# The moving columns of the projections read alternately from two halves of the tokens, in a two-layer decoder trunk

## The chip, the cores and the metric

The kernel runs on one core of one Trainium2 chip. The metric is the device time of one execution in microseconds (us); several runs are given by their median. A profile is one execution recorded by the hardware profiler, with the engines TensorE (PE for its matmuls, PEld for its weight loads), VectorE (DVE), ScalarE (ACT), GpSimd (POOL) and SyncE (SP, which issues the DMAs).

## The reference

16 learned tokens are put ahead of 256 given ones, so that 272 tokens of width 2048 go through two layers. Layer 0 mixes tokens by RWKV-7, layer 1 by gated linear attention (GLA); each is followed by a squared-ReLU MLP with 8192 hidden units. All of it is float32.

```python
h = concatenate([meta, x])                              # 272 x 2048
h = h + rwkv7_time_mix(rms_norm(h))                     # r, k, v, output: 2048 x 2048 each, and low-rank gates
h = h + square(relu(rms_norm(h) @ w1_0)) @ w2_0         # 2048 x 8192, 8192 x 2048
h = h + gla_time_mix(rms_norm(h))                       # w_in 2048 x 6160, w_o 2048 x 2048
h = h + square(relu(rms_norm(h) @ w1_1)) @ w2_1
out = rms_norm(h)[16:]
```

## The kernel before

Activations lie transposed: 128 features on the partitions and the tokens along the free dimension. A projection multiplies weight tiles of 128 by 128 (the stationary operand) with an activation tile (the moving operand, one column for each token) and adds up over the tiles of the contraction in one PSUM bank.

**Two parts of each number.** To keep float32 accuracy with the fast matmul type (`fp32r`), each operand is split into a rounded part and its remainder. An activation tile `x` or `h` is `[128, 2, 272]`: index 0 the rounded part, index 1 the remainder. `wload` (L127 to L139) brings 128 by 1024 weights, eight tiles, by DMA into one of three `raw` buffers; ACT rounds them into one of two `hi` buffers (L137), and DVE writes the remainder into one of two `lo` buffers (L138). One such load is called a group here. It is issued with a high priority, so that it stands early in the queues of SP, ACT and DVE; what it waits for is that the matmuls of the group two before are done with the buffer.

**Two forms of a projection.** `mm3` (L141 to L145, called by `proj`) takes three matmuls for each weight tile: `hi` by the rounded columns, `hi` by the remainder, `lo` by the rounded columns, mostly with all 272 tokens, into one bank of which 272 columns are used. `projw` (L161 to L173) is for the 256 tokens that remain needed late in the kernel. It takes two matmuls: `hi` by rounded part and remainder together, 2 times 256 columns, which fills the bank (L171), and `lo` by the 256 rounded columns (L172) on top of the first half of the bank. The two halves of the bank are added afterwards: by `joined` (ACT copies one half to SBUF, L180; DVE adds the other, L181) or by `addto` (two DVE additions into the residual `hres`, L186). All these matmuls read and write their columns one after the other. Two banks, both called `pj`, take turns.

**Stages in order of time.** The opening computes the first half of r, with eight banks at once, in an order written by hand (L338 to L431, `manual_schedule`). While its first inputs arrive, some matmuls on a tile of ones, `ar`, run into a bank `pu` that nobody reads (L340, and L351 to L360). They use several patterns of 512 moving columns. In L352 to L358 the 512 columns are cut into two halves, and the matmul reads `blk` columns from the first half, `blk` from the second, and so on in turn, for `blk` of 1, 4 and 16, three matmuls each; L360 reads 512 neighbouring columns, from column 1 on, three times:

```python
            for blk in (1, 4, 16):
                x = w[:, :512].rearrange("p (a b c) -> p b a c", a=2, c=blk)
                o = idle.rearrange("p (b a c) -> p b a c", a=2, c=blk)
                ...
                for _ in range(3):
                    nc.tensor.matmul(o, w[:, :128], x, start=True, stop=True)
            for _ in range(3):
                nc.tensor.matmul(idle, w[:, :128], w[:, 1:513], start=True, stop=True)
```

Up to about 640 us follow the rest of RWKV: r, the low-rank gates (`proj32` in plain float32, L198), k with the building of the recurrence's operands, then v and the output projection. The last two are cut into steps, and a hand-written order on TensorE interleaves them with the recurrence (`R(n)` runs n steps). The MLP of layer 0 (to about 1,310 us) is `proj` throughout, with all 272 tokens. GLA (to about 1,820 us) uses both forms, and the MLP of layer 1 (`up` L239, `down` L254) uses `projw`.

Of the kernel before, what the change touches and what calls it, by code (L numbers as in the profile page):

```python
# [13 lines left out]
ALU = mybir.AluOpType  # L14
# [6 lines left out]
KT = D // P  # L21
NMETA = 16
SEQ = 256
T = NMETA + SEQ
# [10 lines left out]
HK = 256  # L35
# [19 lines left out]
class Kern:  # L55
# [71 lines left out]
    def wload(self, src, prio=2000):  # L127
# [11 lines left out]
        return hi, lo  # L139

    def mm3(self, out, hi, lo, ws, xh, xl, first, last):  # L141
        nc = self.nc
        nc.tensor.matmul(out, hi[:, ws], xh, start=first, stop=False)  # L143
        nc.tensor.matmul(out, hi[:, ws], xl, start=False, stop=False)  # L144
        nc.tensor.matmul(out, lo[:, ws], xh, start=False, stop=last)  # L145

    def proj(self, srcs, x, n, off=0, bank=None):
        ps = bank() if bank else self.pj()
        nk = 8 * len(srcs)
        for i, s in enumerate(srcs):  # L150
            hi, lo = self.wload(s)
            for j in range(8):
                kt = 8 * i + j
                xt = x[kt]
                self.mm3(ps[:, :n], hi, lo, slice(j * P, (j + 1) * P), xt[:, 0, off : off + n],
                         xt[:, 1, off : off + n], kt == 0, kt == nk - 1)
        return ps[:, :n]

    def projw(self, srcs, x, off=0):  # L161
        nc = self.nc
        ps = self.pj()
        wide = ps.rearrange("p (a t) -> p a t", a=2)
        nk = 8 * len(srcs)
        for i, s in enumerate(srcs):
            hi, lo = self.wload(s)
            for j in range(8):
                kt = 8 * i + j
                ws = slice(j * P, (j + 1) * P)  # L170
                nc.tensor.matmul(wide, hi[:, ws], x[kt][:, :, off : off + SEQ], start=kt == 0, stop=False)  # L171
                nc.tensor.matmul(ps[:, :SEQ], lo[:, ws], x[kt][:, 0, off : off + SEQ], start=False, stop=kt == nk - 1)  # L172
        return ps[:, :SEQ], ps[:, SEQ:]  # L173


    def joined(self, pool, halves):
        nc = self.nc
        a, b = halves
        c = self.t(pool, [P, SEQ], "cj", 2)
        nc.scalar.copy(c, b)  # L180
        nc.vector.tensor_tensor(out=c, in0=a, in1=c, op=ALU.add)  # L181
        return c

    def addto(self, h, halves):
        for a in halves:
            self.nc.vector.tensor_tensor(out=h, in0=a, in1=h, op=ALU.add)  # L186
# [45 lines left out]
    def mlp(self, layer, x, rstd, hres, off, done):  # L232
        nc, tc, ap = self.nc, self.tc, self.ap
        n = T - off
        w1, w2 = ap[f"mlp_w1_{layer}"], ap[f"mlp_w2_{layer}"]
        with ExitStack() as es:
            hp = es.enter_context(tc.tile_pool(name=f"hid{layer}", bufs=1, side="right", reuse_waits="tile"))

            def up(b):  # L239
                hid = []  # L240
                for f in range(KT):
                    src = [w1[b * KT + f, i] for i in range(2)]
                    ps = self.joined(hp, self.projw(src, x)) if n == SEQ else self.proj(src, x, n)
                    z = self.t(hp, [P, T], "z", 2)[:, :n]
                    nc.vector.scalar_tensor_tensor(out=z, in0=ps, scalar=0.0, in1=rstd, op0=ALU.max, op1=ALU.mult)
# [24 lines left out]
    def rwkv(self, done):  # L270
        nc, tc, ap = self.nc, self.tc, self.ap
        tt = lambda o, a, b, op=ALU.mult: nc.vector.tensor_tensor(out=o, in0=a, in1=b, op=op)  # L272
        hres = self.hres
# [64 lines left out]
        with tc.manual_schedule(engines={ENG.PE, ENG.DVE, ENG.Activation}):  # L338
# [12 lines left out]
            w = warm.bitcast(F32R)  # L351
            for blk in (1, 4, 16):  # L352
                x = w[:, :512].rearrange("p (a b c) -> p b a c", a=2, c=blk)
                o = idle.rearrange("p (b a c) -> p b a c", a=2, c=blk)
                if blk == 1:
                    x, o = x[:, :, :, 0], o[:, :, :, 0]
                for _ in range(3):
                    nc.tensor.matmul(o, w[:, :128], x, start=True, stop=True)  # L358
            for _ in range(3):
                nc.tensor.matmul(idle, w[:, :128], w[:, 1:513], start=True, stop=True)  # L360
            om0 = self.one_minus(ep, "mix0")
# [34 lines left out]
            for kt in range(KT):  # L396
# [20 lines left out]
                for p in parts:  # L417
                    nc.scalar.copy(hi[:, p], raw[:, p])
                    if kt in (0, KT - 1):
                        low(w, p)  # L420
                xh, xl = xr[kt][:, 0], xr[kt][:, 1]
                for f in range(4):
                    nc.tensor.matmul(pss[f], hi[:, cols(f)], xh, start=kt == 0, stop=False)
                for f in range(4):
                    nc.tensor.matmul(pss[f], hi[:, cols(f)], xl, start=False, stop=False)
                    nc.tensor.matmul(pss[f], lo[:, cols(f)], xh, start=False, stop=kt == KT - 1)
                if kt in (0, KT - 1):
# [6 lines left out]
        for f in range(NR):  # L434
            nc.scalar.copy(rr[f], pss[f])
        xw = mix32(1, ep)
        xa = mix32(4, ep)
        tc.keep_in_program_order(nc.scalar.preload_act_table_set("sigmoid_and_others"))
        for f in (NR, NR + 1):
            nc.scalar.copy(rr[f], self.proj(pair(wr, f), xr, T))  # L440
        tw = self.t(e2, [P, T], "tw")
# [18 lines left out]
        for f in range(NR + 2, KT):  # L460
            nc.scalar.copy(rr[f], self.proj(pair(wr, f), xr, T))
# [81 lines left out]
        for f in range(KT):  # L543
# [7 lines left out]
            nc.scalar.activation(iW, ca[:, 0], AF.Exp, scale=DECAY)  # L551
            nc.scalar.mul(kk, ps, self.vec("k_k", f))
            nc.scalar.activation(sq, kk, AF.Square)
# [4 lines left out]
            nc.scalar.activation(sq, sq, AF.Exp, scale=-0.5)  # L558
            tt(kn, ps, kn)
            nc.vector.scalar_tensor_tensor(out=kk, in0=sq, scalar=1e12, in1=kk, op0=ALU.min, op1=ALU.mult)  # L560
# [228 lines left out]
        def v_proj(f):  # L789
            ps = self.pj()[:, :T]  # L790
            yield from units(xv, 2, ps)
            nc.scalar.copy(hres[:, f], ps)
            tt(rr[f], rr[f], hres[:, f])
            yield

        def outA(f):
            ps = self.pj()[:, :T]
            nc.sync.dma_start(loc[f], ap["hT"][:, f])
            yield from units(yo, 1, ps)
            tt(loc[f], ps, loc[f], ALU.add)  # L800
            yield


        def outQ(s, fp):
            hi, lo = weights.pop(0)
            pss = [self.pj()[:, :T] for _ in range(2)]
            for i in range(2):
# [3 lines left out]
                for j in range(4):  # L811
# [4 lines left out]
                    if j < 3:  # L816
                        yield
                tt(hres[:, f] if s == 3 else loc[f], pss[i], loc[f], ALU.add)
                if s == 3:
# [141 lines left out]
    def gla(self, x, rstd, hres, done):  # L961
# [16 lines left out]
        zf = self.t(gp, [P, T], "mn", 2)  # L978
        tt(zf, self.proj(pair(48), x, T), rstd)
        za = self.t(gp, [P, T], "za", 1, F32R)  # L980
# [6 lines left out]
        for hd in range(GH):  # L987
            Q = self.t(gp, [P, 2, 7 * C], "Q", 2)
            KX = self.t(gp, [P, 2, 160 + 6 * C], "KX", 1)
            for dt in range(2):  # L990
# [24 lines left out]
                qf = self.t(gp, [P, SEQ], "qf", 2)  # L1015
                nc.vector.scalar_tensor_tensor(out=qf, in0=pq, scalar=HK ** -0.5, in1=rs, op0=ALU.mult, op1=ALU.mult)
                tt(q[:, : 3 * C], qf[:, : 3 * C], eb[:, c0:c3])
# [7 lines left out]
                ks = self.t(gp, [P, T], "ks", 2)  # L1025
                tt(ks, pk, rstd)
                kx = KX[:, dt]
# [14 lines left out]
            for v in range(4):  # L1042
                pv = self.proj(pair(16 + 4 * hd + v), x, T)
                vs = self.t(gp, [P, T], "vs", 2)
                tt(vs, pv, rstd)
                pt = self.ptr()
# [8 lines left out]
            def cols(x, i, n=1):  # L1055
                return x[:, i * C : (i + n) * C]
# [32 lines left out]
            for v in range(4):  # L1089
                j = 4 * hd + v  # L1090
                pg = self.joined(gp, self.projw(pair(32 + j), x, NMETA))
                gt = self.t(gp, [P, SEQ], "gt", 2)
                tt(gt, pg, rs)
                sg = self.t(gp, [P, SEQ], "sg", 2)
# [155 lines left out]
```

## Time and profile before

| | |
|---|---|
| median of 3 runs | 2545.72 us (2544.17 to 2549.93) |
| profiled execution | 2546.85 us, of which the span from first to last instruction is 2545.1 us |
| mean granted TensorE clock | 0.997 of full speed |
| busy, share of the span | matmuls 99%, weight loads 92%, DVE 65%, ACT 49%, POOL 0% |
| DMA | 455 MB, mean 179 GB/s |

Matmuls are pipelined: a row's duration (289 ns for 272 columns) is that of one instruction from end to end, while the next starts much sooner. The pace of TensorE is read from the distance of two starts, or from a stretch of time divided by the number of matmuls in it. In the rows of the view by windows, each engine's busy time is followed by its count of instructions; the last three figures are the granted clock, the share of DMA time and GB/s.

### The profile page before, as it was taken

The numbers are of one execution on the slowest core, as the hardware profiler recorded it, in microseconds if no ns is written. First come the engines' busy times: TensorE is split into PE (matmuls) and PEld (weight loads), VectorE is DVE, ScalarE is ACT, GpSimd is POOL, SyncE is SP. The second block draws the span as 40 slices with busy tenths as digits, with TensorE's granted clock in tenths as the row PEclk, the third lists the DMA queues.
The fourth block names the chain that finished last, engine by engine and source line by source line (L and its number), as shares of the span: only waits on it lengthen the run. The fifth ranks groups of instructions, "written<-read, shape, count | busy, mean of one in ns | idle before, by whom it ended". The sixth has DMA issues, their size and how long they took to land. (4 is left out here: it accounts for less than half of the span.)

```text
span 2545.1 us, 47169 instructions
## 1 busy us (share of the span) xinstructions
PE 2511.8 (99%) x19262; PEld 2337.6 (92%) x19262; DVE 1643.9 (65%) x2748; ACT 1243.6 (49%) x1951; POOL 6.7 (0%) x20
## 2 busy tenths in 40 slices
PE   9999999999999999999999999999999999999998
PEld 8889998899999999999999999998888888888887
DVE  8777986748555455455456688777666656656665
ACT  6366544555444344344344455545555435445344
POOL 0000000000000000000000000000000000000000
PEclk9999999999999999999999999999999999999999
DMA  6578854434555555555555554445555555555554
GB/s 208 167 233 277 264 153 141 129 103 155 175 177 175 175 177 179 174 175 177 178 175 181 166 169 155 157 149 182 184 189 190 187 187 190 189 186 188 191 188 160
DMA packets 160729, 455.29 MB, mean 179 GB/s; under 512 B 34112, under 2 KB 50624, under 8 KB 160512
## 3 DMA queue, kind: packets, MB, share of 16 engines
q1 hardware_dynamic: 160512, 452.27, 54.9%
q8 instruction: 151, 2.47, 0.4%
q14 instruction: 66, 0.54, 0.1%
HBM read 433.86 MB, written 18.35 MB: 178 GB/s over the span
## 5 line engine op out<-in xcount | busy, mean ns | idle before, releaser
L137 ACT CAST hi<-raw 128x1024 fp32r<-128x1024 f32 (+1 forms) x818 | 796.8, 981 | 1080.6 <-PE pj L144 589.8
L138 DVE TENSOR_TENSOR lo<-raw,hi 128x1024 fp32r<-128x1024 f32 (+1 forms) x818 | 926.7, 1140 | 583.5 <-ACT hi L137 574.7
L143 PE MATMUL pj<-x,hi 128*128 128x272 f32 x2240 | 660.4, 295 | 2.6 <-DVE hres L272 2.5
L145 PE MATMUL pj<-x,lo 128*128 128x272 f32 x2240 | 648.4, 289 | 1.0 <-DVE lo L138 0.9
L144 PE MATMUL pj<-x,hi 128*128 128x272 f32 x2240 | 646.7, 289 | 0.0
L171 PE MATMUL pj<-x,hi 128*128 128x512 f32 x1664 | 585.5, 395 | 2.2 <-DVE cj L181 1.5
L172 PE MATMUL pj<-x,lo 128*128 128x256 f32 x1664 | 468.3, 282 | 1.3 <-DVE lo L138 1.3
L143 PEld LDWEIGHTS pj<-x,hi 128*128 128x128 f32 x2240 | 422.5, 189 | 10.8 <-issue 4.4
L144 PEld LDWEIGHTS pj<-x,hi 128*128 128x128 f32 x2240 | 424.9, 190 | 3.2 <-issue 1.4
L145 PEld LDWEIGHTS pj<-x,lo 128*128 128x128 f32 x2240 | 421.9, 188 | 2.8 <-DVE lo L138 2.1
L171 PEld LDWEIGHTS pj<-x,hi 128*128 128x128 f32 x1664 | 312.5, 188 | 75.6 <-issue 2.1
L171 PE MATMUL pj<-h,hi 128*128 128x512 f32 x1008 | 352.9, 394 | 0.0
L172 PEld LDWEIGHTS pj<-x,lo 128*128 128x128 f32 x1664 | 313.4, 188 | 2.2 <-DVE lo L138 1.9
L143 PE MATMUL pj<-h,hi 128*128 128x272 f32 (+1 forms) x1040 | 299.2, 288 | 0.0
L145 PE MATMUL pj<-h,lo 128*128 128x272 f32 (+1 forms) x1040 | 298.4, 287 | 0.0
L144 PE MATMUL pj<-h,hi 128*128 128x272 f32 (+1 forms) x1040 | 298.1, 287 | 0.0
L172 PE MATMUL pj<-h,lo 128*128 128x256 f32 x1008 | 284.0, 282 | 0.0
L171 PEld LDWEIGHTS pj<-h,hi 128*128 128x128 f32 x1008 | 189.4, 188 | 43.4
L144 PEld LDWEIGHTS pj<-h,hi 128*128 128x128 f32 x1040 | 196.7, 189 | 0.0
L143 PEld LDWEIGHTS pj<-h,hi 128*128 128x128 f32 x1040 | 195.7, 188 | 0.0
L145 PEld LDWEIGHTS pj<-h,lo 128*128 128x128 f32 x1040 | 195.2, 188 | 0.0
L172 PEld LDWEIGHTS pj<-h,lo 128*128 128x128 f32 x1008 | 190.5, 189 | 0.0
(270 smaller groups left out, 2113.7 us busy)
## 6 DMA issues: line engine op xcount, KB each, us to landing
raw<-mlp_w_d SPq DMA_DIRECT2D x512, 512.0 KB, 3.4
raw<-gla_in_d SPq DMA_DIRECT2D x98, 512.0 KB, 3.3
raw<-w_rkv_d SPq DMA_DIRECT2D x80, 512.0 KB, 4.0
raw<-gla_o_d SPq DMA_DIRECT2D x32, 512.0 KB, 3.4
raw<-rw_oQ_d SPq DMA_DIRECT2D x24, 512.0 KB, 3.3
raw<-w_r_d SPq DMA_DIRECT2D x16, 512.0 KB, 3.4
ard<-ar SPq DMA_DIRECT2D x16, 288.0 KB, 3.7
bkd<-bk SPq DMA_DIRECT2D x16, 288.0 KB, 3.8
```

Source lines behind the costliest of these rows:

```text
L137: nc.scalar.copy(hi[:, h], raw[:, h])
L138: nc.vector.tensor_tensor(out=lo[:, h], in0=raw[:, h], in1=hi[:, h].bitcast(F32), op=ALU.subtract)
L143: nc.tensor.matmul(out, hi[:, ws], xh, start=first, stop=False)
L144: nc.tensor.matmul(out, hi[:, ws], xl, start=False, stop=False)
L145: nc.tensor.matmul(out, lo[:, ws], xh, start=False, stop=last)
L171: nc.tensor.matmul(wide, hi[:, ws], x[kt][:, :, off : off + SEQ], start=kt == 0, stop=False)
L172: nc.tensor.matmul(ps[:, :SEQ], lo[:, ws], x[kt][:, 0, off : off + SEQ], start=False, stop=kt == nk - 1)
```

## The change

Every projection in `fp32r` reads its moving columns woven: token 0, token n/2, token 1, token n/2 + 1 and so on, where n is 272 or 256. The distance of the two places is 136 or 128 elements (in the idle matmuls of L358 with `blk` of 1 it is 256). The results are written one after the other as they come, so that the tokens stand woven in the PSUM bank: those of the first half at the even columns, those of the second at the odd ones. Whoever reads the bank, on DVE or ACT, takes every second column, first the even and then the odd ones, and writes the tokens to SBUF in their usual order. No instruction is added or removed outside the idle matmuls, whose twelve patterns are replaced by twelve others. The instructions stand in the same order as before on all engines and queues.

```diff
+    def weave(x):
+        return x.rearrange("p (a t) -> p t a", a=2)
+    def pairs(x):
+        return x.rearrange("p (t a) -> p t a", a=2)
+    def back(x):
+        return x.rearrange("p (t a) -> p a t", a=2)
+    def two(x):
+        return x.rearrange("p (a t) -> p a t", a=2)
 
     def mm3(self, out, hi, lo, ws, xh, xl, first, last):
+        out, xh, xl = self.pairs(out), self.weave(xh), self.weave(xl)
         nc.tensor.matmul(out, hi[:, ws], xh, start=first, stop=False)
 ...
     def proj(self, srcs, x, n, off=0, bank=None):
-        return ps[:, :n]
+        return self.back(ps[:, :n])
 ...
     def projw(self, srcs, x, off=0):
-        wide = ps.rearrange("p (a t) -> p a t", a=2)
+        wide, one = ps.rearrange("p (s t a) -> p s t a", s=2, a=2), self.pairs(ps[:, :SEQ])
 ...
-                nc.tensor.matmul(wide, hi[:, ws], x[kt][:, :, off : off + SEQ], start=kt == 0, stop=False)
-                nc.tensor.matmul(ps[:, :SEQ], lo[:, ws], x[kt][:, 0, off : off + SEQ], start=False, stop=kt == nk - 1)
-        return ps[:, :SEQ], ps[:, SEQ:]
+                xt = x[kt][:, :, off : off + SEQ].rearrange("p s (a t) -> p s t a", a=2)
+                nc.tensor.matmul(wide, hi[:, ws], xt, start=kt == 0, stop=False)
+                nc.tensor.matmul(one, lo[:, ws], xt[:, 0], start=False, stop=kt == nk - 1)
+        return self.back(ps[:, :SEQ]), self.back(ps[:, SEQ:])
 
     def joined(self, pool, halves):
-        nc.scalar.copy(c, b)
-        nc.vector.tensor_tensor(out=c, in0=a, in1=c, op=ALU.add)
-        return c
+        c2 = self.two(c)
+        nc.scalar.copy(c2, b)
+        nc.vector.tensor_tensor(out=c2, in0=a, in1=c2, op=ALU.add)
+        return c2
 
     def addto(self, h, halves):
+        h = self.two(h)
         for a in halves:
             self.nc.vector.tensor_tensor(out=h, in0=a, in1=h, op=ALU.add)
 ...
-            for blk in (1, 4, 16):
-                x = w[:, :512].rearrange("p (a b c) -> p b a c", a=2, c=blk)
 ...
+            for x in (v.rearrange("p (a t) -> p t a", a=4), v.rearrange("p (a t c) -> p t a c", a=2, c=2),
+                      v.rearrange("p (b a t) -> p b t a", a=2, t=16), v.rearrange("p (t a) -> p a t", a=2)):
 ...
+                outs = [self.pairs(x) for x in pss[:4]]
+                xh, xl = self.weave(xh), self.weave(xl)
                 for f in range(4):
-                    nc.tensor.matmul(pss[f], hi[:, cols(f)], xh, start=kt == 0, stop=False)
+                    nc.tensor.matmul(outs[f], hi[:, cols(f)], xh, start=kt == 0, stop=False)
 ...
         for f in range(NR):
-            nc.scalar.copy(rr[f], pss[f])
+            nc.scalar.copy(self.two(rr[f]), self.back(pss[f]))
 ...
-                tt(vs, pv, rstd)
+                tt(self.two(vs), pv, self.two(rstd))
```

The other places where a result is taken out of PSUM (r, k, v, the output projection, the MLP's `z`, GLA's q, k, v and gate) change as the last two do.

More of the change, by code (lines that the diff above doesn't have):

```diff
@@ L139, in wload @@
         return hi, lo
+    @staticmethod
+    def weave(x):
+        return x.rearrange("p (a t) -> p t a", a=2)
+    @staticmethod
+    def pairs(x):
+        return x.rearrange("p (t a) -> p t a", a=2)
+    @staticmethod
+    def back(x):
+        return x.rearrange("p (t a) -> p a t", a=2)
+    @staticmethod
+    def two(x):
+        return x.rearrange("p (a t) -> p a t", a=2)
     def mm3(self, out, hi, lo, ws, xh, xl, first, last):
         nc = self.nc
+        out, xh, xl = self.pairs(out), self.weave(xh), self.weave(xl)
         nc.tensor.matmul(out, hi[:, ws], xh, start=first, stop=False)
@@ L244, in up @@
                     z = self.t(hp, [P, T], "z", 2)[:, :n]
-                    nc.vector.scalar_tensor_tensor(out=z, in0=ps, scalar=0.0, in1=rstd, op0=ALU.max, op1=ALU.mult)
+                    nc.vector.scalar_tensor_tensor(out=self.two(z), in0=ps, scalar=0.0, in1=self.two(rstd), op0=ALU.max,
+                                                   op1=ALU.mult)
                     s = self.t(hp, [P, T], "s", 2)[:, :n]
@@ L351, in rwkv @@
             w = warm.bitcast(F32R)
-            for blk in (1, 4, 16):
-                x = w[:, :512].rearrange("p (a b c) -> p b a c", a=2, c=blk)
-                o = idle.rearrange("p (b a c) -> p b a c", a=2, c=blk)
-                if blk == 1:
-                    x, o = x[:, :, :, 0], o[:, :, :, 0]
+            v = w[:, :512]
+            for x in (v.rearrange("p (a t) -> p t a", a=4), v.rearrange("p (a t c) -> p t a c", a=2, c=2),
+                      v.rearrange("p (b a t) -> p b t a", a=2, t=16), v.rearrange("p (t a) -> p a t", a=2)):
+                o = idle.rearrange("p (t a) -> p t a", a=x.shape[2]) if len(x.shape) == 3 else idle.rearrange(
+                    "p (t a c) -> p t a c", a=x.shape[2], c=x.shape[3])
                 for _ in range(3):
                     nc.tensor.matmul(o, w[:, :128], x, start=True, stop=True)
-            for _ in range(3):
-                nc.tensor.matmul(idle, w[:, :128], w[:, 1:513], start=True, stop=True)
             om0 = self.one_minus(ep, "mix0")
@@ L421, in rwkv @@
                 xh, xl = xr[kt][:, 0], xr[kt][:, 1]
+                outs = [self.pairs(x) for x in pss[:4]]
+                xh, xl = self.weave(xh), self.weave(xl)
                 for f in range(4):
-                    nc.tensor.matmul(pss[f], hi[:, cols(f)], xh, start=kt == 0, stop=False)
+                    nc.tensor.matmul(outs[f], hi[:, cols(f)], xh, start=kt == 0, stop=False)
                 for f in range(4):
-                    nc.tensor.matmul(pss[f], hi[:, cols(f)], xl, start=False, stop=False)
-                    nc.tensor.matmul(pss[f], lo[:, cols(f)], xh, start=False, stop=kt == KT - 1)
+                    nc.tensor.matmul(outs[f], hi[:, cols(f)], xl, start=False, stop=False)
+                    nc.tensor.matmul(outs[f], lo[:, cols(f)], xh, start=False, stop=kt == KT - 1)
                 if kt in (0, KT - 1):
@@ L439, in rwkv @@
         for f in (NR, NR + 1):
-            nc.scalar.copy(rr[f], self.proj(pair(wr, f), xr, T))
+            nc.scalar.copy(self.two(rr[f]), self.proj(pair(wr, f), xr, T))
         tw = self.t(e2, [P, T], "tw")
@@ L460, in rwkv @@
         for f in range(NR + 2, KT):
-            nc.scalar.copy(rr[f], self.proj(pair(wr, f), xr, T))
+            nc.scalar.copy(self.two(rr[f]), self.proj(pair(wr, f), xr, T))
             if f == NR + 2:
@@ L551, in rwkv @@
             nc.scalar.activation(iW, ca[:, 0], AF.Exp, scale=DECAY)
-            nc.scalar.mul(kk, ps, self.vec("k_k", f))
+            nc.scalar.mul(self.two(kk), ps, self.vec("k_k", f))
             nc.scalar.activation(sq, kk, AF.Square)
@@ L558, in rwkv @@
             nc.scalar.activation(sq, sq, AF.Exp, scale=-0.5)
-            tt(kn, ps, kn)
+            tt(self.two(kn), ps, self.two(kn))
             nc.vector.scalar_tensor_tensor(out=kk, in0=sq, scalar=1e12, in1=kk, op0=ALU.min, op1=ALU.mult)
@@ L791, in v_proj @@
             yield from units(xv, 2, ps)
-            nc.scalar.copy(hres[:, f], ps)
+            nc.scalar.copy(self.two(hres[:, f]), self.back(ps))
             tt(rr[f], rr[f], hres[:, f])
@@ L799, in outA @@
             yield from units(yo, 1, ps)
-            tt(loc[f], ps, loc[f], ALU.add)
+            tt(self.two(loc[f]), self.back(ps), self.two(loc[f]), ALU.add)
             yield
@@ L817, in outQ @@
                         yield
-                tt(hres[:, f] if s == 3 else loc[f], pss[i], loc[f], ALU.add)
+                tt(self.two(hres[:, f] if s == 3 else loc[f]), self.back(pss[i]), self.two(loc[f]), ALU.add)
                 if s == 3:
@@ L978, in gla @@
         zf = self.t(gp, [P, T], "mn", 2)
-        tt(zf, self.proj(pair(48), x, T), rstd)
+        tt(self.two(zf), self.proj(pair(48), x, T), self.two(rstd))
         za = self.t(gp, [P, T], "za", 1, F32R)
@@ L1015, in gla @@
                 qf = self.t(gp, [P, SEQ], "qf", 2)
-                nc.vector.scalar_tensor_tensor(out=qf, in0=pq, scalar=HK ** -0.5, in1=rs, op0=ALU.mult, op1=ALU.mult)
+                nc.vector.scalar_tensor_tensor(out=self.two(qf), in0=pq, scalar=HK ** -0.5, in1=self.two(rs), op0=ALU.mult,
+                                               op1=ALU.mult)
                 tt(q[:, : 3 * C], qf[:, : 3 * C], eb[:, c0:c3])
@@ L1025, in gla @@
                 ks = self.t(gp, [P, T], "ks", 2)
-                tt(ks, pk, rstd)
+                tt(self.two(ks), pk, self.two(rstd))
                 kx = KX[:, dt]
@@ L1092, in gla @@
                 gt = self.t(gp, [P, SEQ], "gt", 2)
-                tt(gt, pg, rs)
+                tt(self.two(gt), pg, self.two(rs))
                 sg = self.t(gp, [P, SEQ], "sg", 2)
```

## Prediction

> **What bounds the kernel now.** I read the page's busy times, the chain that ended last, the costliest groups, then single stages.
>
> ```profile
> PE 2511.8 (99%) x19262; PEld 2337.6 (92%) x19262; DVE 1643.9 (65%) x2748; ACT 1243.6 (49%) x1951; POOL 6.7 (0%) x20
> PEclk9999999999999999999999999999999999999999
> PE 32%; DVE 1%; ACT 0%; issue 0%; DVEq 0%
> PE pj L171 21%; PE pj L172 11%; DVE fin L1158 0%; DVE lo L138 0%; DVE sg L1097 0%; PE pj L144 0%; PE pj L145 0%; PE pj L143 0%; DVE gt L963 0%; DVE x L963 0%; PE pm L1153 0%; PE pry L1087 0%; PE pm L228 0%; DVE hres L1158 0%; DVEq L1245 0%
> L143 PE MATMUL pj<-x,hi 128*128 128x272 f32 x2240 | 660.4, 295 | 2.6 <-DVE hres L272 2.5
> L145 PE MATMUL pj<-x,lo 128*128 128x272 f32 x2240 | 648.4, 289 | 1.0 <-DVE lo L138 0.9
> L171 PE MATMUL pj<-x,hi 128*128 128x512 f32 x1664 | 585.5, 395 | 2.2 <-DVE cj L181 1.5
> L172 PE MATMUL pj<-x,lo 128*128 128x256 f32 x1664 | 468.3, 282 | 1.3 <-DVE lo L138 1.3
> L171 PE MATMUL pj<-h,hi 128*128 128x512 f32 x1008 | 352.9, 394 | 0.0
> ```
>
> TensorE is the bound: matmuls fill 99% of the span, the chain (followed back only as far as 32% of the span) consists of the two projection lines, and ahead of the projections it idles 0 to 2.6 us in all. The clock is full, so there is nothing to win there. What remains is the pace of a matmul.
>
> ```profile
> core 0: us, PE busy (x) PEld busy (x) DVE busy (x) ACT busy (x) POOL busy (x), PEclk, DMA share, GB/s
> 700.00:900.00 200.00, 200.00 (x1604) 200.00 (x1603) 104.01 (x122) 85.90 (x109) 0.00 (x0) 1.00 0.54 176
> 1900.00:2100.00 200.00, 200.00 (x1145) 174.67 (x1144) 122.25 (x163) 94.64 (x131) 0.00 (x0) 1.00 0.58 187
> ```
>
> From 700 to 900 us, in the MLP of layer 0, all matmuls have 272 columns: 200 us / 1604 = 124.7 ns each, 0.458 ns a column. From 1900 to 2100 us (MLP of layer 1) wide and narrow ones alternate: 2 x 200 / 1145 = 349.3 ns a pair of 512 and 256 columns, 0.455 ns a column.
>
> The trace holds a faster pace. The idle matmuls of the opening stream 512 columns each in four patterns; the rows give the start of one of each pattern.
>
> ```profile
> 11.88 0.59 PE L358 MATMUL pu<-ar 128*128 128x512 f32 x2
> 12.32 0.66 PE L358 MATMUL pu<-ar 128*128 128x512 f32 x2
> 13.07 0.64 PE L358 MATMUL pu<-ar 128*128 128x512 f32 x2
> 13.79 0.62 PE L360 MATMUL pu<-ar 128*128 128x512 f32 x2
> 14.02 0.63 PE L360 MATMUL pu<-ar 128*128 128x512 f32 x2
> ```
>
> At 11.88 starts the second of the three with `blk` of 1, at 12.32 the first with 4, at 13.07 the first with 16, at 13.79 and 14.02 two with neighbouring columns. So two woven matmuls took 0.44 us, 0.22 each (0.43 ns a column; the rounding of two starts leaves 0.215 to 0.225); three with runs of 4 took 0.75, 0.25 each; three with runs of 16 took 0.72, 0.24 each; one of neighbouring columns took 0.23. The pattern that the change gives to all projections is the fastest of the four.
>
> **The change part by part.** *272 columns.* The first two rows below count the L143 matmuls from 63 us on, 927 + 2436 = 3363; each belongs to an `mm3`, so there are 10,089 matmuls, and the opening's 16 weight tiles by 8 features by 3 add 384: 10,473.
>
> ```profile
> 63.00:640.00 577.00, 282.72 (x927) 175.28 (x926) 0.99 0.58 180
> 640.00:2545.00 1905.00, 701.09 (x2436) 458.09 (x2435) 1.00 0.54 178
> 120.00:640.00 520.00, 263.86 (x863) 163.34 (x863) 0.99 0.59 182
> 0.00:2545.00 2545.00, 938.16 (x2672) 501.87 (x2672) 1.00 0.55 179
> ```
>
> Scaled from 512 columns at 0.215 to 0.22 us, 272 would take 114 to 117 ns. A fixed part in each matmul would push this up and the weight load, one with every matmul, may set a floor. How short a load can get shows in the present narrow matmul:
>
> ```profile
> 2006.37 0.19 PEld L171 LDWEIGHTS pj<-h,hi 128*128 128x128 f32 x1
> 2006.49 0.19 PEld L172 LDWEIGHTS pj<-h,lo 128*128 128x128 f32 x1
> 2006.48 0.39 PE L171 MATMUL pj<-h,hi 128*128 128x512 f32 x1
> ```
>
> The load for the wide matmul starts at 2006.37 and that matmul starts 0.11 us later, so a load needs 0.12 at most. Bounds are 114 and 120 ns; I take 116, near the scaled value, since the columns are what sets today's pace. That is 8.7 ns by 10,473 = 91 us.
>
> *Pairs of 512 and 256.* The last row above counts 2672. The wide one goes to 216 ns. The narrow one scales to 108 to 110, and the load bounds it by 120; today it takes what 349.3 leaves beside some 231, about 118. I take 110. A pair then takes 326 ns, 23.3 less, by 2672 = 62 us. Together 153 us, if TensorE stays the bound everywhere.
>
> *RWKV, 120 to 640 us.* Of the 10,473, 3 x 863 = 2,589 lie here, worth 22.5 us. Here others are near their limits:
>
> ```profile
> 220.00:240.00 20.00, 19.96 (x154) 18.97 (x154) 13.63 (x32) 12.39 (x22) 0.00 (x0) 1.00 0.92 308
> 300.00:320.00 20.00, 20.00 (x173) 19.46 (x173) 19.45 (x45) 7.06 (x15) 0.00 (x0) 1.00 0.93 294
> 320.00:480.00 160.00, 152.94 (x2244) 138.16 (x2244) 113.72 (x282) 78.49 (x162) 3.33 (x6) 0.98 0.52 148
> ```
>
> At 300 us DVE is busy 19.45 of 20 us, at 220 us the DMA engines 92%, and from 320 us on the projections fill the waits of the recurrence, which shorter matmuls fill less well. Between all and nothing I take half: 11 us are lost.
>
> *Reading PSUM with a step of two.* No row shows this. It may cost nothing, even gain a little; as the other end I let every element count twice, by the DVE row with 512 elements from PSUM against the one with 256.
>
> ```profile
> L186 DVE TENSOR_TENSOR hres<-pj,hres 128x256 f32<-128x256 f32 x159 | 67.5, 425 | 52.5 <-PE pj L172 46.7 <-PE pj L145 3.2
> L272 DVE TENSOR_TENSOR S<-pu,WC 128x512 f32<-128x512 f32 x8 | 5.5, 684 | 4.2 <-PE pu L722 4.2
> 2006.57 1.05 ACT L137 CAST hi<-raw 128x1024 fp32r<-128x1024 f32 x1 [1.75 <-PE pj L171]
> 2006.68 0.89 DVE L186 TENSOR_TENSOR hres<-pj,hres 128x256 f32<-128x256 f32 x2 [0.61 <-PE pj L172]
> 2007.65 1.23 DVE L138 TENSOR_TENSOR lo<-raw,hi 128x1024 fp32r<-128x1024 f32 x1
> 2009.28 0.39 PE L171 MATMUL pj<-h,hi 128*128 128x512 f32 x1
> DVE hres L186 <- PE pj L172: 46.7, 79, 0.7
> ```
>
> That is 684 - 425 = 259 ns for each read. Most of it is covered: a bank is next written one projection (over 5 us) later, and DVE is idle 39% of the stage. The tight place is `down` with `projw`. There the two `addto` reads end at 2007.57, and `lo`, queued behind them, starts at 2007.65 when `hi` is ready; it ends at 2008.88 for a group that starts at 2009.28, a reserve of 0.40 us. The faster group takes 8 x 23.3 = 0.19 us of it, leaving 0.21, so at the present cost of a read nothing waits. With the doubled cost `lo` is late by 2 x 0.26 - 0.08 = 0.44: TensorE waits 0.23 us, 79 times (the last row), 18 us. I take 4 us, nearer to nothing, since the DVE fetches one element at a time as it is (259 ns for 256 elements). The Trainium skill warns here (Vector Engine (DVE) Microarchitecture Reference, section 5.2, Measured stream behaviour on trn2): a stream keeps its full pace in runs of at least two neighbouring words, and costs about 1.7 to 2.5 ns a column where each element hops, against 1.05. That was measured in SBUF; no run here shows it for PSUM. By it, as an estimate, a read would cost some 0.18 to 0.37 us more and the sum would lose 8 to 40 us here instead of 4.
>
> ACT's reads (L180, the r and v copies) have their cover in ACT's 51% idle time. The faster groups ask for 7% more weights a second, 187 to some 200 GB/s in the MLP, below the 308 at 220 us. The new idle matmuls run before the first inputs are ready and cost nothing.
>
> Sum: 2546.85 - 153 + 11 + 4 = 2409 us for the profiled execution; the median of the runs is 1.1 us below it, so **2408 us**.
>
> **The rivals.** *The weave does not hold at the new distance.* In the idle matmuls the two places lie 256 elements apart, here 136 or 128, and the tile there is small and always the same. If changing place costs here what it cost with runs of 4, a column takes 0.25 / 512 = 0.488 ns: 272 columns take 133 ns (8 more, 10,473 times: 84 us), a pair 375 (26 more, 2672 times: 68 us), and the kernel takes about 2700 us. The switch lies at 124.7 ns for 272 columns. Against it speaks that hopping after every column was the cheapest of the hopping patterns. The Trainium skill takes this side (Advanced Engine Details and Errata, Memory Cachelines): SBUF lines have 16 bytes, and a stream that goes to another line with each access pays a penalty. The trace does not agree, with 0.22 us woven against 0.23 of neighbours. 0.11.
>
> *The weight load is the floor.* With 120 ns for every load, 272 columns gain 4.7 ns (49 us) and a pair 349.3 - 216 - 120 = 13 (35 us): 84 less 15 is 69, or 2477 us. With a floor of 118 it would be 70 + 41 - 15 = 96, or 2450. For it: loads are busy 200 of 200 us in the MLP. Against it: that counts durations of 188 ns that overlap. 0.12.
>
> *The step-of-two reads are slow.* At the doubled cost 18 us instead of 4, and some 8 more in RWKV, where DVE is full (k and v, 32 reads by 0.26): about 2430 us. 0.2.
>
> *No change in pace:* the weave reads as neighbours do, 2545 us. 0.03.
>
> **How the numbers follow.** The forecast has 0.54; it and the slow reads, both faster, span from 2380 (all of the 153 us and a few more where a narrow matmul reaches 108) to some 2435. I carry the upper end to 2455 to take in the milder floor. What is left out: the weave failing, no change, and the harder floor, under 2 in 10. A difference of 0.2%, 5 us, is about what a measurement of this kernel can tell from none: its runs lie within 0.23%. Faster 0.86, same 0.03, slower 0.11.
>
> **What would show it.** In the MLP of layer 0 some 1,720 matmuls in 200 us instead of 1604, and in that of layer 1 some 1,227 instead of 1145. The `addto` row should stay near 425 ns; 684 would be the slow read, and PE would then show idle time ahead of L172 put down to `lo`. Fewer than 1604 matmuls in the first stretch would prove the forecast wrong by its main term; 1604 to 1660 would point to the load.

## The result, and the profile after

The changed kernel takes 2420.34 us (median of 4 runs, 2418.27 to 2422.38) against 2547.82 us of the kernel before beside it: a ratio of 0.949 with a 95% interval of 0.946 to 0.953, 5.1% faster. The forecast was 2408 us, in a range of 2380 to 2455.

First the page of the changed kernel: span, busy times, and the costliest matmul groups. Line numbers have moved: `mm3` is L160 to L162 now, `projw` L189 and L190, `addto` L206.

```profile
span 2419.9 us, 47169 instructions
PE 2371.1 (98%) x19262; PEld 2235.7 (92%) x19262; DVE 1640.0 (68%) x2748; ACT 1242.5 (51%) x1951; POOL 6.6 (0%) x20
PEclk9999999999999999999999999999999999999999
PE pj L189 21%; PE pj L190 10%; DVE fin L1180 0%; DVE lo L138 0%; DVE sg L1119 0%; PE pj L161 0%; PE pj L160 0%; PE pj L162 0%; DVE gt L984 0%; DVE x L984 0%; PE pm L1175 0%; PE pm L248 0%; PE pry L1109 0%; DVE hres L1180 0%; DVEq L1267 0%
L162 PE MATMUL pj<-x,lo 128*128 128x272 f32 x2240 | 631.4, 282 | 5.8 <-DVE lo L138 5.6
L189 PE MATMUL pj<-x,hi 128*128 128x512 f32 x1664 | 550.5, 384 | 3.8 <-ACT hi L137 3.0
L190 PE MATMUL pj<-x,lo 128*128 128x256 f32 x1664 | 457.0, 275 | 1.6 <-DVE lo L138 1.5
```

The span lost 125.2 us. Instruction counts are equal, DVE and ACT are busy about as long as before (1640.0 us now and 1643.9 before, 1242.5 and 1243.6), and the mean granted clock is 0.996 of full speed now and 0.997 before. The saving is on TensorE alone. It still idles little, but ahead of `mm3`'s third matmul (L162, before L145) 5.8 us in place of 1.0, nearly all of it waiting for `lo`. Its pace shows in the view by windows, for the MLP of layer 0, that of layer 1, and GLA:

```profile
core 0: us, PE busy (x) PEld busy (x) DVE busy (x) ACT busy (x) POOL busy (x), PEclk, DMA share, GB/s
700.00:900.00 200.00, 200.00 (x1729) 200.00 (x1728) 111.17 (x128) 90.12 (x112) 0.00 (x0) 1.00 0.58 190
1850.00:2050.00 200.00, 200.00 (x1224) 183.97 (x1223) 131.16 (x176) 102.32 (x144) 0.00 (x0) 1.00 0.61 201
1336.00:1739.00 403.00, 394.00 (x2729) 365.33 (x2727) 315.39 (x568) 217.58 (x354) 0.00 (x0) 1.00 0.52 171
```

200 / 1729 = 115.7 ns for 272 columns (124.7 before), and 2 x 200 / 1224 = 326.8 ns a pair (349.3). By these paces, with 10,464 matmuls and 2672 pairs, the change was worth 94 + 60 = 154 us. So 29 us were not collected. The next table says where. The stages are bounded by the starts of the matmul that begins an RMS norm (L228 before, L248 after) and by the last matmul; "by the pace" is 9.0 ns for each matmul of `mm3` and 22.5 for each pair in the stage. By these bounds the MLP of layer 0 ends at 1,399 us in the kernel before (632.3 + 767.2), not at 1,310 as the description of the stages has it; an expectation below that counts GLA as 490 us takes in the end of this MLP.

| stage | before, us | after, us | gained | by the pace |
|---|---|---|---|---|
| RWKV | 632.3 | 621.8 | 10.5 | 27.9 |
| MLP of layer 0 | 767.2 | 713.4 | 53.8 | 55.3 |
| GLA | 419.1 | 404.1 | 15.0 | 25.2 |
| MLP of layer 1, end | 715.8 | 670.0 | 45.8 | 45.9 |

The MLPs collected nearly everything (53.8 of 55.3 us, 45.8 of 45.9), RWKV 38%, GLA 60%. Two questions follow: what makes the woven columns faster, and what holds RWKV and GLA.

### The profile page after: what moved, and what is told of

The parts are those of the page before. It is cut to its first block, busy times and chain, and to the rows that moved or that the text cites. A ratio compares the mean times of both kernels' runs of the same rounds, so it can differ in the third digit from the quotient of the medians.

```text
span 2419.9 us, 47169 instructions
## 1 busy us (share of the span) xinstructions
PE 2371.1 (98%) x19262; PEld 2235.7 (92%) x19262; DVE 1640.0 (68%) x2748; ACT 1242.5 (51%) x1951; POOL 6.6 (0%) x20
## 5 line engine op out<-in xcount | busy, mean ns | idle before, releaser
L160 PE MATMUL pj<-x,hi 128*128 128x272 f32 x2240 | 640.7, 286 | 4.4 <-DVE hres L293 2.8
L162 PE MATMUL pj<-x,lo 128*128 128x272 f32 x2240 | 631.4, 282 | 5.8 <-DVE lo L138 5.6
L161 PE MATMUL pj<-x,hi 128*128 128x272 f32 x2240 | 628.2, 280 | 0.0
L189 PE MATMUL pj<-x,hi 128*128 128x512 f32 x1664 | 550.5, 384 | 3.8 <-ACT hi L137 3.0
L190 PE MATMUL pj<-x,lo 128*128 128x256 f32 x1664 | 457.0, 275 | 1.6 <-DVE lo L138 1.5
L160 PEld LDWEIGHTS pj<-x,hi 128*128 128x128 f32 x2240 | 424.3, 189 | 12.6 <-issue 4.7
L162 PEld LDWEIGHTS pj<-x,lo 128*128 128x128 f32 x2240 | 424.3, 189 | 10.7 <-DVE lo L138 9.6
L189 PEld LDWEIGHTS pj<-x,hi 128*128 128x128 f32 x1664 | 315.3, 189 | 48.0 <-ACT hi L137 3.7
L189 PE MATMUL pj<-h,hi 128*128 128x512 f32 x1008 | 330.3, 382 | 0.0
L190 PEld LDWEIGHTS pj<-x,lo 128*128 128x128 f32 x1664 | 320.1, 192 | 4.6 <-DVE lo L138 4.1
L160 PE MATMUL pj<-h,hi 128*128 128x272 f32 (+1 forms) x1040 | 290.1, 279 | 0.0
L161 PE MATMUL pj<-h,hi 128*128 128x272 f32 (+1 forms) x1040 | 290.1, 279 | 0.0
L162 PE MATMUL pj<-h,lo 128*128 128x272 f32 (+1 forms) x1040 | 290.1, 279 | 0.0
L190 PE MATMUL pj<-h,lo 128*128 128x256 f32 x1008 | 274.8, 273 | 0.0
L189 PEld LDWEIGHTS pj<-h,hi 128*128 128x128 f32 x1008 | 190.5, 189 | 26.4
L160 PEld LDWEIGHTS pj<-h,hi 128*128 128x128 f32 x1040 | 196.6, 189 | 0.0
L162 PEld LDWEIGHTS pj<-h,lo 128*128 128x128 f32 x1040 | 196.6, 189 | 0.0
L190 PEld LDWEIGHTS pj<-h,lo 128*128 128x128 f32 x1008 | 193.5, 192 | 0.0
```

The costliest lines, as they stand in the source:

```text
L189: nc.tensor.matmul(wide, hi[:, ws], xt, start=kt == 0, stop=False)
L190: nc.tensor.matmul(one, lo[:, ws], xt[:, 0], start=False, stop=kt == nk - 1)
```

## Experiments

**One form at a time.** The first kernel leaves `projw` as it was, the second leaves `mm3` as it was:

```diff
 # mm3 only, in projw:
-        wide, one = ps.rearrange("p (s t a) -> p s t a", s=2, a=2), self.pairs(ps[:, :SEQ])
+        wide, one = ps.rearrange("p (a t) -> p a t", a=2), ps[:, :SEQ]
 ...
 # projw only, in mm3:
-        out, xh, xl = self.pairs(out), self.weave(xh), self.weave(xl)
 ...
```

The reads of the bank change with it: of the form that is left as it was, they take the first half of the columns and then the second.

> Only the matmuls of mm3 are woven; projw reads its columns one after the other as before. If the two forms gain independently, the 272-column matmuls run at 115.7 ns and a pair stays at 349 ns: the MLP of layer 0 is 9% shorter as in the full change, that of layer 1 as long as before; the span is 2545 - 94 + some 20 lost to waits in RWKV and GLA = 2465 to 2480 us. If the shorter time comes from something else in the changed kernel (the order, the evacuation), both MLPs move or neither.

> Only projw is woven. Independent gains: 124.7 ns for 272 columns, 327 ns for a pair, span 2545 - 60 + some 8 = 2488 to 2495 us. The losses in RWKV, where no projw runs, should be gone: there the time is as before (about 640 us).

They took 2471.52 and 2491.55 us (one run each, both in the expected range), beside 2544.97 for the kernel before. By stages, `mm3` only: RWKV 620.1, MLP of layer 0 712.5, GLA 411.0, MLP of layer 1 715.5. `projw` only: 632.5, 767.1, 409.2, 670.3. Each form saves in its own stages and nothing elsewhere. In the MLPs the savings are those of the whole change within 1 us; in GLA they are 8.1 and 9.9 us, 18.0 together, where the whole change saved 15.0, so that something there gives less the faster TensorE gets. Reading the bank in two halves brings nothing by itself: with unwoven matmuls and such reads the MLPs take 767.1 and 715.5 us, as before.

**What the pace hangs on.** The idle matmuls of the changed kernel's opening were replaced by 17 patterns, three matmuls each:

```diff
+            tests = [(v, idle), (w[:, 1:513], idle)]
 ...
+            for t in (64, 16, 8, 4, 2):
+                tests.append((v.rearrange("p (b a t) -> p b t a", a=2, t=t), idle.rearrange("p (b t a) -> p b t a", t=t, a=2)))
+            tests.append((v.rearrange("p (a t c) -> p t a c", a=2, c=8), idle.rearrange("p (t a c) -> p t a c", a=2, c=8)))
+            tests.append((v.rearrange("p (t a) -> p a t", a=2), idle.rearrange("p (a t) -> p a t", a=2)))
 ...
```

> The changed kernel with other idle matmuls in the opening: 17 patterns, three of each; the span grows by up to 8 us and says nothing. If the pace hangs on the distance of the two places, short distances (8, 4, 2 columns) are slower than 256; if it hangs on going through two places in turn at all, all distances of 8 and more give 0.216 us for 512 columns, and 4 and 2 are in doubt. Neighbouring columns give 0.230 to 0.234 for 512, 0.125 for 272, 0.118 for 256, from an even or an odd start, woven ones 0.116 for 272 and 0.109 for 256. If the side that writes PSUM set the pace, neighbouring columns written in runs of 2 or 8 to two places in turn would be slower than 0.234; if the reading side does, they stay at 0.230 to 0.234. Every second column, read alone, took 0.44 in the changed kernel and should again.

The kernel took 2435.66 us (one run), 15 us more than the changed kernel, where up to 8 were expected. It lies in RWKV (638.0 us, 16 more): 7 us are the longer row of idle matmuls; the rest is not explained (from 340 to 480 us the granted clock is 0.94, and 0.96 in the changed kernel). The MLP of layer 0 (712.4 us) is as in the changed kernel.

The trace of this kernel, weight loads of the opening, at a granted clock of 1.00. In these rows a load starts when the matmul ahead of it starts, so that each row here stands for the start of the first of three equal matmuls.

```profile
12.29 0.19 PEld L386 LDWEIGHTS pu<-ar 128*128 128x128 f32 x1
13.00 0.19 PEld L386 LDWEIGHTS pu<-ar 128*128 128x128 f32 x1
13.73 0.19 PEld L386 LDWEIGHTS pu<-ar 128*128 128x128 f32 x1
14.38 0.19 PEld L386 LDWEIGHTS pu<-ar 128*128 128x128 f32 x1
17.65 0.19 PEld L386 LDWEIGHTS pu<-ar 128*128 128x128 f32 x1
18.30 0.19 PEld L386 LDWEIGHTS pu<-ar 128*128 128x128 f32 x1
18.99 0.19 PEld L386 LDWEIGHTS pu<-ar 128*128 128x128 f32 x1
19.72 0.19 PEld L386 LDWEIGHTS pu<-ar 128*128 128x128 f32 x1
21.05 0.21 PEld L386 LDWEIGHTS pu<-ar 128*128 128x128 f32 x1 [0.24 <-issue]
21.78 0.19 PEld L386 LDWEIGHTS pu<-ar 128*128 128x128 f32 x1
```

Three matmuls of 512 neighbouring columns (from column 1 on) took 12.29 to 13.00, 0.235 us each. Woven at a distance of 256 elements: 13.73 to 14.38, 0.217 each. At a distance of 4 elements, 16 bytes: 17.65 to 18.30, 0.217. At a distance of 2 elements: 18.30 to 18.99, 0.23, as neighbours read. In runs of 8: 18.99 to 19.72, 0.243. Every second column, then the others: 19.72 to 21.05, 0.44. Neighbouring columns that are written in runs of two to two places in turn: 21.05 to 21.78, 0.24; in runs of eight, 0.23. The distances 64, 16 and 8 also gave 0.216, and the start on an odd column made no difference to either. As in the projections, 272 columns took 0.126 as neighbours and 0.115 woven, 256 columns 0.118 and 0.111.

So it is the reading side: two places in turn, at each distance that was run from 4 elements (16 bytes) up, while 2 elements (8 bytes) bring nothing. How the columns are written matters little. Why two places are read faster than neighbours no run shows. The changed kernel's own idle matmuls add that more places or more columns at a time spoil it: four places in turn took 0.28, two columns from each of two places 0.34:

```profile
12.10 0.73 PE L379 MATMUL pu<-ar 128*128 128x512 f32 x2
12.67 0.85 PE L379 MATMUL pu<-ar 128*128 128x512 f32 x2
13.35 0.72 PE L379 MATMUL pu<-ar 128*128 128x512 f32 x2
```

The first row is the second of the four-place pattern (two of them take 0.57 us to the next row), the second is the first with pairs, and the third row its third (two take 0.68).

**What holds GLA.** TensorE idled 1.0 us ahead of three of the q projections, 0.5 us in the kernel before; the view puts these waits down to `hi` now, and to the read of a bank by DVE (`cj`) before. One reason could be that q needs the PSUM bank that DVE has not yet read; the other that DVE has more to do there than fits. The bank is tested by giving k's projection another one:

```diff
-                pk = self.proj(pair(8 + j), x, T)
+                pk = self.proj(pair(8 + j), x, T, bank=self.pu)
```

> The changed kernel with GLA's k projection in the bank pu, which is free there, so that the q projection after it need not wait until its pj bank has been read. Theory of the wait for a bank: the gaps of about 1.3 us ahead of the q projections (seven of them) go, GLA is 5 to 9 us shorter. Theory of the full DVE: DVE's work in that stretch is the same, TensorE waits for lo instead, and GLA is within 3 us of the changed kernel's 490 us.

The kernel took 2415.43 us (one run), GLA 401.1 us. Of the five kernels with unchanged GLA two took 401.6 and 401.7, and three, the changed kernel among them, 404.1 to 404.7. These three alone have a stretch near 1,657 us with a lower granted clock, 0.83 in the mean of 10 us; in the changed kernel:

```profile
1655.00:1665.00 10.00, 7.92 (x36) 6.43 (x35) 6.20 (x11) 5.01 (x8) 0.00 (x0) 0.83 0.33 106
```

The kernel with the other bank has none, so its like are the two of 401.6 and 401.7, and the bank brought about 0.5 us, or nothing. TensorE's wait moved as the second theory had it: the idle time ahead of the q projections is gone, and ahead of the load for L190 it waited for `lo` 6.2 us in place of 4.1. The views of the weight loads' waits in GLA, changed kernel and then this one, where the wait for `hi` is no longer among the longest:

```profile
PEld pj L190 <- DVE lo L138: 4.1, 11, 1.6
PEld pj L189 <- ACT hi L137: 3.7, 4, 1.2
```

```profile
PEld pj L190 <- DVE lo L138: 6.2, 15, 1.6
```

Then DVE was relieved. The first kernel moves the reciprocals of the gates to ACT (16 of 1746 ns, 28 us), by a logarithm and an exponential where ACT added 1 before: one operation more for each, 1967 in all in place of 1951, while the expectation has their number unchanged; the second moves four small copies and scalings too.

```diff
-                nc.scalar.activation(sg, sg, AF.Identity, bias=1.0)
-                nc.vector.reciprocal(out=sg, in_=sg)
+                nc.scalar.activation(sg, sg, AF.Ln, bias=1.0)
+                nc.scalar.activation(sg, sg, AF.Exp, scale=-1.0)
```

> The changed kernel with GLA's 16 reciprocals on DVE (1746 ns each, 28 us) replaced: ACT takes ln(1+e) and then exp of its negative, where it took 1+e before; ACT's count of operations is the same. Theory of the full DVE: the stretch at the turn of each head where DVE was busy 19.7 of 20 us loses part of its backlog, and GLA gets 4 to 10 us shorter, most of the 11.4 us that it fell short by. Theory that the matmuls' latency chains or banks set GLA's time: under 2 us.

> As the one before, and four small copies and scalings for each q/k pair go from DVE to ACT (some 0.6 us of DVE time, eight times). Theory of the full DVE: another 2 to 5 us off GLA, TensorE's idle time in GLA falls from some 14 us to under 6. Otherwise within 1 us of the one before, or longer, because ACT now makes hi wait.

They took 2412.02 us (ratio 0.947, 0.944 to 0.950) and 2411.05 us (0.946, 0.944 to 0.949), and GLA 395.1 and 394.4 us: 9.0 and 9.7 us less than in the changed kernel, but 6.5 and 7.2 less than in the two kernels with unchanged GLA whose clock stayed full there, as it did here. By the pace alone GLA would take 393.9. The reciprocals bought nearly all of it, with 20 us less of busy time on DVE in all (1619.9 in place of 1640.0); the small pieces added 0.7, less than the 2 to 5 expected. The windows of one head's turn, about 28 us from the group of the first q projection on: before, after, and with the reciprocal moved:

```profile
1480.00:1510.00 30.00, 29.49 (x204) 27.59 (x203) 29.41 (x69) 18.23 (x32) 0.00 (x0) 1.00 0.53 175
```

```profile
1413.00:1441.00 28.00, 26.84 (x193) 25.14 (x193) 27.73 (x63) 17.98 (x32) 0.00 (x0) 1.00 0.56 177
```

```profile
1410.00:1438.00 28.00, 27.80 (x205) 26.36 (x204) 25.90 (x64) 18.54 (x34) 0.00 (x0) 1.00 0.58 188
```

The third number of busy time is DVE's: 29.4 of 30 us before the change, 27.7 of 28 after. DVE was full here in the first place, so a faster TensorE only idled more (26.84 of 28 busy). Without the reciprocals DVE has 2.1 us free and TensorE does 205 matmuls where it did 193. That DVE held GLA is shown; of the 10 us lost there some 2.5 go with the lower clock near 1,657 us instead. Whether the kernel before would have gained by the same edit was not run.

Both edits of GLA and the other bank together:

> The changed kernel with the reciprocals and the small copies of GLA on ACT and k's projection in the bank pu. If DVE is what holds GLA, the bank adds under 1 us to the 394 us of GLA that the ACT version took: 2408 to 2413 us in all. If the bank is a wait of its own once DVE is relieved, 389 to 392.

2410.97 us (0.947, 0.946 to 0.949), GLA 393.8: the bank adds no more than 0.6 us, as expected of DVE, and the time is that of the kernel without it (2411.05) within the spread of the runs.

**What holds RWKV.** First suspicion: DVE again, with the steps of the triangular inverse.

```diff
-                tt(w, X[:n, s : s + 1, s + 1 :].to_broadcast([n, m, k]), X[:n, :m, s : s + 1].to_broadcast([n, m, k]))
-                tt(X[:n, :m, s + 1 :], X[:n, :m, s + 1 :], w, ALU.add)
```

> The kernel before without the 30 steps of products and sums of the triangular inverse in RWKV on DVE (the inverse is left out, so what the recurrence gets is wrong); its four passes of some 20 us of DVE work each, that share the stretch from 280 to 600 us with the projections, are gone. The MLPs are as before. It is the base for the next run: RWKV takes 620 to 640 us.

> The changed kernel without the same steps. RWKV up to 640 us gained only 11.0 of 28.4 us. Theory that DVE is full there: against the run before, RWKV now gains over 17 us, the more so after 280 us. Theory that TensorE's in-order queue meets short dependent matmuls (the sums by head in the k loop, the recurrence) whose operands take their time whatever the load: the gain stays 9 to 14 us, and the shortfall before 280 us, where no inverse runs, stays about 8.

The kernels took 2543.86 and 2416.99 us (one run each), RWKV 629.3 us before and 619.4 after the change: 9.9 gained, against 10.5 with the inverse and over 17 if DVE's work on it were the limit. RWKV in kernels that leave it as the change has it takes 618.8 to 622.2 us. The inverse's work on DVE is not what holds it.

Second suspicion: the sums by head in the k loop, whose operands come from ACT and DVE while TensorE stands at them in its order. In both kernels they got the operand of the feature before, so that k and the bonus term are not the right ones:

```diff
-            nc.tensor.matmul(ss, self.bones, sq, start=True, stop=True)
+            nc.tensor.matmul(ss, self.bones, early_of[0] if f else sq, start=True, stop=True)
 ...
-            nc.tensor.matmul(rk, self.bones, kn, start=True, stop=True)
+            nc.tensor.matmul(rk, self.bones, early_of[1] if f else kn, start=True, stop=True)
+            early_of = sq, kn
```

> The kernel before, with the two sums by head in RWKV's k loop (32 matmuls of ones) taking the operand of the feature before instead of their own, so that TensorE need not wait for ACT and DVE in the middle of a group; what k and the bonus term get is wrong. All instructions are there. It is the base for the next run. The stretch from the first of these sums to the first matmul of the recurrence's centring, 175.0 us before, gets shorter by up to 8 us if these waits are exposed.

> The changed kernel with the same edit. In the stretch named above the change gained 2.4 us (175.0 to 172.6) of 9.8 that its matmuls should give. Theory of the dependent matmuls in TensorE's in-order queue: with the waits gone in both, the change gains 6 to 10 us here. Theory of DMA or DVE as the limit of this stretch (DMA 84% busy, DVE 92% after 250 us): it gains 1 to 4 us as before, and TensorE waits for weights or lo instead.

The kernels took 2543.07 and 2420.49 us (one run each). The stretch took 172.5 us before and 172.6 after: no gain at all, where the pace would give 9.8 us. The waits went (TensorE on `sq`: 2.5 us, five times, to 1.4, once), and others came in their place, `lo` and data behind it. The waits on TensorE from 168 to 340 us, changed kernel and then this one:

```profile
PE pm L577 <- ACT sq L574: 2.5, 5, 0.9
PE pj L162 <- DVE lo L138: 2.1, 2, 1.0
```

```profile
PE pj L162 <- DVE lo L138: 4.0, 8, 1.4
PE pt L522 <- DMA BK<-bkd: 3.2, 1, 3.2
```

For the sums by head the theory of dependent matmuls falls: with these waits gone, plain and woven columns take the same time, and it is the time of the changed kernel with the waits (171.3 to 173.0 us in the six kernels that leave RWKV as the change has it; 176.7 in the kernel of the patterns, which is longer in all of RWKV). Something other than the pace of the matmuls sets it. A weight load lands after 4.3 us here in the median, and after 3.4 in the MLPs, though 4.2 in one stretch of them (700 to 900 us). All DMAs of the stretch, the stores of each feature among them, stand in one queue of SP. The last run issued those stores one feature later, on top of the edit before:

```diff
-            nc.sync.dma_start(bkd[f], bk)
-            nc.sync.dma_start(ard[f], ar)
+            if f:
+                nc.sync.dma_start(bkd[f - 1], st2[0][(f - 1) % 2])
+                nc.sync.dma_start(ard[f - 1], st2[1][(f - 1) % 2])
 ...
```

> As the changed kernel with the sums by head taking the operand of the feature before (what k and the bonus term get is wrong), and the two stores of each feature's operands issued one feature later, when their data has long been ready, so that the weight loads behind them in SP's queue need not wait for DVE. The bytes moved are the same. In the run without this second edit the stretch from the first sum by head to the first centring matmul stayed at 172.6 us. If SP's order held the weights back: under 169 us. If the DMA engines' bandwidth (84% busy, 270 GB/s) or DVE's own work does: 171 to 174 us.

172.3 us, and 2418.55 for the kernel (one run). But it settles little: the scheduler kept the stores close to where they had been, and SP still waited for DVE ahead of one of them, 18.2 us in the stretch where it had waited 17.6 without the edit:

```profile
SPq L570 <- DVE ar L586: 18.2, 8, 3.7
```

What limits this part of RWKV, the rate of the DMA engines (81% busy, 256 GB/s), SP's order behind DVE, or DVE's other work, stays open. That it is not the waits at the sums by head is shown.

The stretch accounts for 7.4 of the 17.4 us that RWKV lost. Some 4.8 were lost ahead of it and 5.1 behind it, and no run looks for the cause there. Two rows of the changed kernel name candidates: in the opening DVE is busy 45.84 of 46 us, and from 320 to 480 us the granted clock is 0.97, where it was 0.98 before.

```profile
24.00:70.00 46.00, 44.82 (x373) 43.69 (x372) 45.84 (x98) 31.46 (x63) 0.00 (x0) 1.00 0.54 181
320.00:480.00 160.00, 151.07 (x2277) 135.68 (x2276) 114.57 (x284) 79.84 (x165) 3.31 (x6) 0.97 0.53 150
```

## Why the prediction held, and where its terms were off

- **TensorE's pace is the bound, and the idle matmuls of the opening give the new one.** Right, and the whole gain. 272 columns were put at 116 ns and take 115.7; a pair was put at 326 and takes 326.8. The sum of 153 us was 154, with 10,464 matmuls in place of the 10,473 counted.
- **The distance of the two places.** The rival that the weave would not hold at 136 or 128 elements fell; the distances of 4, 8, 16, 64 and 256 elements give one pace, and so do 136 and 128 in the projections. The rule of the Trainium skill against lines visited in turn (Advanced Engine Details and Errata, Memory Cachelines) does not hold for two of them, 0.217 us against 0.235 of neighbours; with four places, 0.28, the trace agrees with it.
- **The weight load as a floor.** Not there at the rival's price: a narrow matmul, with a load of its own, has come to about 110 ns (326.8 less the 217 of a wide one), where 118 to 120 was the rival's price.
- **Reading PSUM with a step of two.** Put at 4 us, with up to 18 as the other end. It cost nothing. The row of `addto` after the change, and the copies of `joined` on ACT before and after it:

```profile
L206 DVE TENSOR_TENSOR hres<-pj,hres 128x256 f32<-128x256 f32 x159 | 67.5, 425 | 39.5 <-PE pj L190 33.7 <-PE pj L162 2.8
L180 ACT COPY cj<-pj 128x256 f32<-128x256 f32 x88 | 32.1, 365 | 0.0
L199 ACT COPY cj<-pj 128x256 f32<-128x256 f32 x88 | 32.4, 368 | 0.0
```

  425 ns as before, and 368 against 365 on ACT. (The estimate of 8 to 40 us comes out as 6 to 36 by the prediction's own steps, 79 times the time by which `lo` would be late.) The rule of the Trainium skill on single words (Vector Engine (DVE) Microarchitecture Reference, section 5.2, Measured stream behaviour on trn2) does not carry over from SBUF to these reads.
- **RWKV.** Put at a loss of 11 us, half of what the matmuls there could give; it lost 17. The direction was right, the size of the term was not. Of the reasons given, DVE's full stretch at 300 us is not it: without the inverse DVE is busy 10.5 of those 20 us, and RWKV is no shorter than in the other kernels (619.4 us).
- **GLA.** The step that failed: no loss was put there at all, and 10 us were lost. The prediction shows no stretch of GLA by itself, and over GLA as a whole DVE seems to have room, busy 317 of 418 us before the change:

```profile
1400.00:1818.00 418.00, 412.63 (x2728) 377.82 (x2727) 317.05 (x567) 216.71 (x353) 0.00 (x0) 1.00 0.51 165
```

  The turn of a head, where it was busy 29.4 of 30 us, was in the trace but was not looked at.

The terms off are 6 us in RWKV, 10 in GLA and 4 the other way for the reads. That makes about the 12 us between 2408 and 2420. That the range held them is in part luck: what it has above 2408 was kept for slow reads of PSUM (to some 2435) and for a floor of the weight load (to 2455), neither of which came, and not for a loss in GLA.

## What to carry to other kernels

When the bound engine is made faster, the gain is the pace times the count only where nothing else is full; look for the others' busiest 30 us in each stage, not for their mean over the stage. A loss that is proven to come from a full engine is also an offer: here one operation moved from DVE to ACT, 16 times, made GLA 6.5 to 9 us shorter, and the whole kernel 8.3 us by the medians (2420.34 to 2412.02). And a pattern that a trace holds by chance, in matmuls that compute nothing, can be the best evidence for an edit there is.

## What the runs showed of the hardware

A matmul of 512 `fp32r` columns from SBUF takes 0.235 us with neighbouring columns, and 0.217 when two places take turns, at distances of 4, 8, 16, 64 and 256 elements. At 2 elements the gain is gone (0.23); with two columns at a time or four places the stream is slower than either (0.34, 0.28); every second column takes 0.44. DVE and ACT read 256 float32 values from PSUM with a step of two as fast as without it (425 and 425 ns, 368 and 365).
